# An eighth set of block products in a hybrid decoder layer: the first branch's other merge gates, and where the partner halves stand

## The chip, the core and the metric

The kernel runs on one core of one Trainium2 chip. The time is device microseconds (us) of one execution. A core has TensorE (PE, with its weight loads as PEld), VectorE (DVE), ScalarE (ACT), GpSimd (POOL) and SyncE (SP), each with an instruction queue of its own that it works off in order, and 16 DMA engines that all queues share. DMAs are issued from the queues of SP and POOL here, a few from ACT.

## The reference

One decoder layer over 256 tokens of width 2048, all in float32:

```python
h = rmsnorm(x, pre_norm_g)
proj = h @ w_in                       # 2048 x 18448
(a_q, a_k, a_v, a_g, a_lr, b_q, b_k, b_v, b_g, m_a, m_b) = split(proj)
gk  = log_sigmoid(a_lr @ gla_gk_w2 + gla_gk_b) / 16
o_a = gla_chunked(a_q, a_k, a_v, gk)              # gated linear attention, 4 heads
y_a = (rmsnorm(o_a, gla_norm_g) * silu(a_g)) @ w_branch_a
o_b = diff_attention(b_q, b_k, b_v, lam)          # 16 heads, two softmaxes each
y_b = (rmsnorm(o_b, diff_norm_g) * 0.8 * silu(b_g)) @ w_branch_b
merged = sigmoid(m_a) * y_a + sigmoid(m_b) * y_b
x = x + rmsnorm(merged @ w_out, post_norm_g)
```

`m_a` and `m_b` are the merge gates of the first and the second branch, 2048 columns each.

## The kernel before

**Splitting.** Nearly all the work is weights streamed from HBM against resident activations. Every weight tile comes in halves of 128x1024. For each half ACT writes a rounded copy `hi` (line 261), DVE the remainder `lo` (line 262), and PE multiplies `hi` by both parts of the activations and `lo` by the first. `hi` and `lo` have three buffers each; `take` lets ACT and DVE run three halves ahead of PE (`AHEAD`), in the order of one list, `seq`.

**Three kinds of half.** A plain token-major half (`half_tile`, 512 columns) is 12 matmuls of 512 columns. A channel-major half (`half_channel`) is 8 matmuls of 512 and 8 of 256 columns. Half of a block product is 6 matmuls of 512 columns.

**Sets of block products.** Seven groups of 1024 columns (`set0` to `set6`) are multiplied as 2x2 blocks by seven products in place of eight (`block_products`): the tokens in two blocks of 128, the 2048 rows of the weights in two of 1024, the columns in two of 512. The products run in the order 1, 3, 5, 6, 2, 7, 4, each in two steps t = 0, 1 of two halves: 14 steps or 28 halves a set. Sums of activation blocks are made once. Sums of weight blocks are made per set, in the tiles `chain[s, "a", t]` and `chain[s, "b", t]` of 1 MiB each:

- `link` loads a and b. Four buffers serve them, so the next set's a0 waits until DVE has read b0 in step (7,0), its a1 for step (7,1), b0 for (4,0) and b1 for (4,1). All but the first set's are issued from POOL (line 175).
- After step (1,t) has been split, an accumulating DMA from POOL (line 198, 512 KB) adds another weight block to each half of a[t]. Steps (5,0) and (5,1) need that sum.
- In steps (5,1), (6,0), (2,1), (7,0) DVE adds b or a third block `c` to a (line 206), and after (5,1) and (6,0) a second accumulating DMA adds to b, for product 7.
- The `c` tiles, four of 512 KB a set, are loaded by SP (line 190) ahead of product 2.

Finished gates leave the core to DRAM (`spill`, tiles `gr` and `gl`, line 129).

**Partner halves.** Between the steps stand halves of other projections, `others()`: the last value columns `v4`, then q and k of the first branch, then q and k of the second one's head groups (`dq`, `dk`) for the groups in `EARLY`, at most one half after a step (two in four steps of set 0). `phase_steps` writes this list; it leaves 14 steps without a partner, product 2's and 4's first steps in sets 1 to 6 and product 6's in sets 1 and 2. Each partner tile (`raw`, 1 MiB, two halves) is loaded by SP into one of three buffers (line 224). The time of this phase of sets is 85 to 593 us of the profile.

**After the phase** come the gates of the first branch (`ag0` to `ag3`), the first branch's merge gates `m02` and `m03` as plain groups of 512 columns around head group 3's channel-major halves (`diff_heads(3)`), then the two branch matrices and the output matrix. The attention of both branches runs as generators (`tasks`) that `pump` advances between these halves.

**Order.** The instructions of the phase's matmuls are pinned (`keep_in_program_order`); elsewhere a scheduler may move an instruction within its engine's queue, the fetches from DRAM among them (`fetch` line 134, `place` line 951).

Of the kernel before, what the change touches and what calls it, by code (L numbers as in the profile page):

```python
# [10 lines left out]
AF = mybir.ActivationFunctionType  # L11
# [3 lines left out]
P = 128  # L15
# [9 lines left out]
LANES = 3  # L25
# [1 line left out]
ROWS = {"two": 2, "tok": 4, "chan": KT}  # L27
WARM = 8
PRODUCTS = (1, 3, 5, 6, 2, 7, 4)
SETS = 7  # L30
MERGE = (0, 1, 6)
LEAD = 6
EARLY = (0, 1, 2)
BIG = 18
MORE = 13
BRIDGE = 512
# [3 lines left out]
def chunk_plan():  # L40

    plan = [("v0", "two", "w_in", [(6144, RANK), (2048, 2 * VG[0] - RANK)])]
    at = 2 * VG[0] - RANK
    for g, n in enumerate(VG[2:]):
        plan.append((f"v{g + 2}", "tok", "w_in", [(2048 + at, n)]))
        at += n
    for hf in range(2):
        for name, base in (("k", 1024), ("q", 0)):
            for c in range(4):
                plan.append((f"{name}{hf}{c}", "chan", "w_in", [(base + 512 * hf + P * c, P)]))  # L50
    o = 6144 + RANK
    for s in range(2):
        plan.append((f"set{s}", "set", "w_in", [(o + 10240 + 1024 * s, 1024)]))
    for s in range(2, 6):
        plan.append((f"set{s}", "set", "w_in", [(o + base + 512 * (s - 2), 512) for base in (4096, 6144)]))
    plan.append(("set6", "set", "w_in", [(o + 8192, 1024)]))
    for g in range(4):
        plan.append((f"ag{g}", "tok", "w_in", [(4096 + 512 * g, 512)]))
        for c in range(4):
            for n, name in enumerate(("dq", "dk")):  # L60
                plan.append((f"{name}{g}{c}", "chan", "w_in", [(o + 2048 * n + 512 * g + P * c, P)]))
        if g > 1:
            plan.append((f"m0{g}", "tok", "w_in", [(o + 8192 + 512 * g, 512)]))
        for br in range(2):
            plan.append((f"y{br}{g}", "tok", ("w_branch_a", "w_branch_b")[br], [(512 * g, 512)]))
        plan.append((f"o{g}", "tok", "w_out", [(512 * g, 512)]))
    return plan
# [9 lines left out]
def phase_steps():  # L77

    keys = ["v4"] + [f"{name}{hf}{c}" for hf in range(2) for name in ("k", "q") for c in range(4)]
    keys += [f"{name}{g}{c}" for g in EARLY for pair in range(2) for name in ("dq", "dk") for c in (2 * pair, 2 * pair + 1)]  # L80
    other = [(key, r, h) for key in keys for r in range(4 if key == "v4" else 1) for h in range(2)]
    slots = [(s, prod, t) for s in range(SETS) for prod in PRODUCTS for t in range(2)]
    front = [(0, prod, t) for prod in PRODUCTS[:2] for t in range(2)]
    skip = [(s, prod, 0) for prod in (2, 4, 6) for s in range(1, SETS)]
    skip = skip[: len(slots) + len(front) - len(other)]
    mixed = []
    for slot in slots:
        mixed += [("set", *slot, h) for h in range(2)]
        for _ in range((slot not in skip) + (slot in front)):
            mixed.append(other.pop(0))  # L90
    return mixed + other
# [3 lines left out]
def hybrid_kernel(ctx: ExitStack, tc, xt, xn, preg, postg, w, w2, gkb, glag, lamv, diffg, ident_d, causal_d, lmask_d, out):  # L95
    nc = tc.nc
    pe, act, dve, pool, sp = nc.tensor, nc.scalar, nc.vector, nc.gpsimd, nc.sync
# [28 lines left out]
    def spill(t, name):  # L126
        count[0] += 1
        d = dram.tile(list(t.shape), t.dtype, name=f"{name}_{count[0]}")
        pool.dma_start(d, t)
        return d  # L130

    def fetch(d, name, make, queue=pool):
        t = make(list(d.shape), name, d.dtype)
        queue.dma_start(t, d)
        return t

    def ps(tag):
# [3 lines left out]
    def f32(ap):  # L141
        return ap.bitcast(F32)
# [10 lines left out]
    def halves_of(*keys):  # L153
        return [(key, r, h) for key in keys for r in range(len(at[key])) for h in range(2)]

    def heads_order(g):
        return halves_of(*(f"{name}{g}{c}" for pair in range(2) for name in ("dq", "dk") for c in (2 * pair, 2 * pair + 1)))

    seq = halves_of("v0", "v2", "v3") + phase_steps()
    seq += halves_of(*(f"ag{g}" for g in range(4)))  # L160
    seq += halves_of("m02") + heads_order(3) + halves_of("m03", *(f"y0{g}" for g in range(4)))
    seq += halves_of(*(f"{name}{g}" for name in ("y1", "o") for g in range(4)))
    ready = {}
    emitted = [0]
# [13 lines left out]
    def emit_set(s, prod, t, h):  # L178
        c = slice(1024 * h, 1024 * h + 1024)
        if h == 0 and s + 1 < SETS and (prod, t) in ((7, 1), (4, 0)):  # L180
            link(s + 1, "a", 1 - t)
        if h == 0 and s + 1 < SETS and (prod, t) == (4, 1):
            link(s + 1, "b", 0)
# [161 lines left out]
    half_rstd = const.tile([P, 2], F32, name="half_rstd")  # L345
# [53 lines left out]
    ts, heads, m0 = {}, {}, []  # L399
# [63 lines left out]
    def token_major(key, n, ops, step=1, settle=None):  # L463
        banks = [ps("mm"), ps("mm")]
        for q in range(KT // 2):
            if settle:
                settle(q)
            half_tile(banks, n, q, ops, *take(key))
            if q % 2 or not ts:
                pump(step)  # L470
            else:
                pump_eager()
        return banks
# [179 lines left out]

    gspill = [None] * (2 * SETS)

    def merge_gate(banks):
        t = u2([P, 2, 512], "mgate")
        for b in range(2):
            act.activation(t[:, b, :], banks[b], AF.Tanh, scale=half_rstd[:, b : b + 1])
        m0.append(spill(t, "mgate"))  # L660

    def head_part(t, o, o2, scaled):
        act.activation(t, o2, AF.Copy)
        dve.tensor_tensor(out=t, in0=o, in1=t, op=ALU.add)
# [115 lines left out]

    sets = (step for s in range(SETS) for step in block_products(s))
    rest = others()
# [165 lines left out]
    obh, obl, values = [], [], {}  # L948

    def place(t, d, m, h):  # L950
        sp.dma_start(f32(t[64 * h : 64 * h + 64, m]), d[64 * m : 64 * m + 64])

    waiting = [(g, pair) for g in range(4) for pair in range(2)]

# [139 lines left out]
    for g in range(4):  # L1094
        banks = token_major(f"ag{g}", 512, x_ops, LANES)
        t = u2([P, 2, 512], "ua")
# [4 lines left out]
    def diff_heads(g):  # L1101
        for pair in range(2):
            for name in ("dq", "dk"):
                t = t2([P, 2, S], name)
                for c in range(2):
                    head_part(t[:, c, :], *channel_major(f"{name}{g}{2 * pair + c}"), name == "dk")
                    pump(LANES)
                heads[g, pair, name] = split_spill(t)
# [7 lines left out]
    def b_ops(kt):  # L1116
        return obh[kt // 4][:, kt % 4, :], obl[kt // 4][:, kt % 4, :]

    m0.extend(gspill[12:14])
    merge_gate(token_major("m02", 512, x_ops, LANES))  # L1120
    diff_heads(3)
    merge_gate(token_major("m03", 512, x_ops, LANES))

    while "out" not in done:
        pump(LANES)
# [1 line left out]
    for g in range(4):  # L1127
        part = fetch(m0[g], "part", u)
        banks = token_major(f"y0{g}", 512, a_ops, LANES)
# [29 lines left out]
    for g in range(4):  # L1159
        banks = token_major(f"y1{g}", 512, b_ops, 1 if g else LANES, None if g else settle)  # L1160
        for b in range(2):
            t = gb[g][:, b, :]
# [51 lines left out]
    for g in range(3):  # L1214
        banks = token_major(f"o{g}", 512, m_ops)
# [88 lines left out]
```

## Time and profile before

| | us |
|---|---|
| median of 3 runs (lowest, highest) | 1107.81 (1106.69, 1108.84) |
| the profiled execution, and its span | 1113.69, 1111.9 |
| PE busy | 1095.0 of the span (98%) |
| DVE, ACT, POOL busy | 863.4, 680.5, 132.3 |
| DMA: bytes moved, mean rate | 274.57 MB, 247 GB/s |

The profiled execution took 5.9 us more than the median run. Shares of busy time are means over the whole span; the rows for single stretches are shown with the prediction. A row of a group reads: line, engine, operation, written tile, read tiles, shapes, count, then busy us, mean ns of one, then the idle time before and what ended it.

### The profile page before, as it was taken

Reading aid. Unit: us, or ns where it says so; the run is one execution under the profiler, and the core shown is the slowest. Engines: PE = TensorE matmul, PEld = TensorE weight load, DVE = VectorE, ACT = ScalarE, POOL = GpSimd, SP = SyncE. Lnnn points to the kernel's source line nnn. Section 1 sums busy time; section 2 is a strip of 40 time slices with the busy share of each in tenths; the row PEclk is TensorE's granted clock in tenths of the full one; section 3 lists DMA queues with packets and bytes.
Section 4 is the critical chain, followed back from the end, with each engine's and each line's share of the span. In section 5 each row is a group of like instructions: output and inputs, shape, how many; then the busy total and the mean of one; then the engine's idle time right before and its main releaser. Section 6 shows DMA issues by size and latency. Waiting matters only on the chain.

```text
span 1111.9 us, 15248 instructions
## 1 busy us (share of the span) xinstructions
PE 1095.0 (98%) x5522; PEld 939.9 (85%) x5522; DVE 863.4 (78%) x1200; ACT 680.5 (61%) x989; POOL 132.3 (12%) x201
## 2 busy tenths in 40 slices
PE   8999999999999999999999999999999999999997
PEld 7999888888888888888887788888888888888886
DVE  6787987979979899798895998668877765656463
ACT  7895766666666666676664655557776653444460
POOL 0101112121121211213111000110110010000000
PEclk9999999999999999999999899999999999999999
DMA  8869969798897997988977445886888675556752
GB/s 329 296 225 325 297 241 319 204 309 222 285 298 204 340 252 264 314 211 317 269 244 249 146 160 187 271 277 228 273 288 243 206 260 189 190 189 212 272 197 76
DMA packets 58268, 274.57 MB, mean 247 GB/s; under 512 B 7824, under 2 KB 9360, under 8 KB 39248
## 3 DMA queue, kind: packets, MB, share of 16 engines
q1 hardware_dynamic: 36192, 184.18, 47.0%
q0 software_dynamic: 20992, 88.09, 28.6%
q10 hardware_dynamic: 1008, 1.32, 0.4%
q8 instruction: 43, 0.70, 0.2%
q14 instruction: 33, 0.27, 0.1%
HBM read 248.40 MB, written 25.17 MB: 246 GB/s over the span
## 4 chain that ended last, share of the span: by engine, by line
PE 94%; DMA 1%; issue 1%; ACT 1%; DVE 1%; POOL 0%; DVEq 0%; SPq 0%; POOLq 0%; ACTq 0%
PE mm L449 62%; PE bg L449 21%; PE bg L437 2%; PE mm L422 2%; PE mm L437 2%; PE bg L862 1%; DMA dl<-dk 1%; PE bg L422 1%; PE bg L996 1%; PE bg L997 1%; DMA raw<-in_w_dram 0%; PE bg L1021 0%; DVE lo L262 0%; PE bg L1034 0%; PE bg L1033 0%
## 5 line engine op out<-in xcount | busy, mean ns | idle before, releaser
L261 ACT ACTIVATE hi<-raw 128x1024 fp32r<-128x1024 f32 (+3 forms) x275 | 282.7, 1030 | 271.0 <-PE mm L449 168.3
L262 DVE TENSOR_TENSOR lo<-raw,hi 128x1024 fp32r<-128x1024 f32 (+3 forms) x275 | 325.9, 1188 | 145.1 <-ACT hi L261 142.0
L449 PE MATMUL mm<-hi,xs 128*128 128x512 f32 (+1 forms) x848 | 216.4, 389 | 4.2 <-ACT hi L261 4.2
L449 PEld LDWEIGHTS mm<-hi,xs 128*128 128x128 f32 x848 | 158.1, 190 | 31.3 <-ACT hi L261 5.0
L449 PE MATMUL bg<-xs,hi 128*128 128x512 f32 x640 | 164.9, 389 | 0.0
L262 DVE TENSOR_TENSOR lo<-a,hi 128x1024 fp32r<-128x1024 f32 x112 | 135.1, 1220 | 10.8 <-ACT hi L261 9.4
L449 PEld LDWEIGHTS bg<-xs,hi 128*128 128x128 f32 x640 | 120.3, 188 | 23.4
L261 ACT ACTIVATE hi<-a 128x1024 fp32r<-128x1024 f32 x112 | 118.7, 1060 | 29.8 <-PE mm L449 24.7
L449 PE MATMUL mm<-lo,xs 128*128 128x512 f32 (+1 forms) x424 | 119.0, 386 | 0.1
L449 PEld LDWEIGHTS mm<-lo,xs 128*128 128x128 f32 x424 | 79.6, 189 | 15.6 <-DVE lo L262 1.0
L449 PEld LDWEIGHTS bg<-xs,lo 128*128 128x128 f32 x640 | 87.3, 190 | 6.2
L449 PE MATMUL bg<-xs,lo 128*128 128x256 f32 x640 | 89.2, 282 | 0.0
L262 DVE TENSOR_TENSOR lo<-b,hi 128x1024 fp32r<-128x1024 f32 x56 | 67.3, 1221 | 7.0 <-ACT hi L261 6.2
L261 ACT ACTIVATE hi<-b 128x1024 fp32r<-128x1024 f32 x56 | 59.2, 1060 | 18.1 <-PE mm L449 15.8
L449 PE MATMUL mm<-hi,oah 128*128 128x512 f32 x128 | 50.9, 397 | 0.0
L449 PE MATMUL mm<-hi,obh 128*128 128x512 f32 x128 | 50.4, 394 | 0.0
L449 PE MATMUL mm<-hi,oal 128*128 128x512 f32 x128 | 50.0, 391 | 0.0
L449 PE MATMUL mm<-hi,obl 128*128 128x512 f32 x128 | 49.9, 390 | 0.0
L1007 ACT ACTIVATE prob<-prob,mx,score_scale 128x128 f32<-128x128 f32 x64 | 34.2, 536 | 13.2 <-DVE mx L1002 13.0
L198 POOL DMA_DIRECT2D b<-in_w_dram x28 | 24.4, 870 | 140.7 <-DVE a L206 127.7
L261 ACT ACTIVATE hi<-c 128x1024 fp32r<-128x1024 f32 x28 | 29.6, 1060 | 13.4 <-PE mm L449 6.8
L449 PE MATMUL mm<-hi,mh 128*128 128x512 f32 x96 | 37.5, 390 | 0.0
(288 smaller groups left out, 1882.3 us busy)
## 6 DMA issues: line engine op xcount, KB each, us to landing
raw<-in_w_dram SPq DMA_DIRECT2D x120, 1024.0 KB, 5.4
a<-in_w_dram POOLq DMA_DIRECT2D x28, 512.0 KB, 14.1
c<-in_w_dram SPq DMA_DIRECT2D x28, 512.0 KB, 8.9
b<-in_w_dram POOLq DMA_DIRECT2D x28, 512.0 KB, 7.7
a<-in_w_dram POOLq DMA_DIRECT2D x12, 1024.0 KB, 5.8
b<-in_w_dram POOLq DMA_DIRECT2D x12, 1024.0 KB, 8.9
raw<-in_w_dram SPq DMA_DIRECT2D x14, 832.0 KB, 6.9
dh<-dh POOLq DMA_DIRECT2D x16, 256.0 KB, 4.1
```

Source lines behind the costliest of these rows:

```text
L198: pool.dma_start(chain[s, name, i][:, c], weights(f"set{s}", 2 + i)[0][:, c], accum_op=ALU.add)
L261: act.activation(hi_t[:, a:b], r[:, a:b], AF.Copy)
L262: dve.tensor_tensor(out=lo_t[:, a:b], in0=r[:, a:b], in1=f32(hi_t[:, a:b]), op=ALU.subtract)
L422: i = pe.matmul(out, lhs, rhs, start=first and n == 0, stop=last and n == len(pairs) - 1)
L437: i = pe.matmul(banks[g][b][:, :n], a[part][:, P * b : P * b + P], w[:, n * g : n * g + n], start=first, stop=last)
L449: i = pe.matmul(*args, **kw)
L862: pe.matmul(o, xk[:, P * c : P * c + P], xq.rearrange("p (b c t) -> p b c t", b=2, c=4)[:, :, c, :], start=i == 0, stop=i == 1)
L996: pe.matmul(banks[m][:, lo:up], q2[:, m, i2, t], kh[:, m, i2, :n], start=True, stop=False)
L997: pe.matmul(banks[m][:, lo:up], q2[:, m, i2, t], kl[:, m, i2, :n], start=False, stop=True)
L1007: act.activation(prob[m][:, lo:up], prob[m][:, lo:up], AF.Exp, scale=score_scale[:, b : b + 1], bias=mx[:, i : i + 1], accum_out=z[:, i : ...
```

## The change

An eighth set takes the columns of `m02` and `m03`, 1024 columns, and these leave the tail as plain groups. Head group 2 leaves `EARLY`: its 16 channel-major halves move from the phase, where they were partners, to the tail, as `diff_heads(2)` behind `ag3`. The list of steps without a partner is rewritten: 44 of 112 steps, in sets 1 to 7 (1,0), (1,1), (3,0), (3,1), (5,0) and (4,0), and in set 7 also (7,1) and (4,1). Fetches and `place` are pinned to program order.

```diff
-SETS = 7
-MERGE = (0, 1, 6)
+SETS = 8
+MERGE = (0, 1, 6, 7)
-EARLY = (0, 1, 2)
+EARLY = (0, 1)
...
-    plan.append(("set6", "set", "w_in", [(o + 8192, 1024)]))
+    for s in range(6, SETS):
+        plan.append((f"set{s}", "set", "w_in", [(o + 8192 + 1024 * (s - 6), 1024)]))
...
-    skip = [(s, prod, 0) for prod in (2, 4, 6) for s in range(1, SETS)]
+    skip = [(SETS - 1, prod, t) for prod, t in ((7, 1), (4, 0), (4, 1))]
+    skip += [(s, prod, t) for prod, t in ((4, 0), (1, 0), (3, 0), (3, 1), (1, 1), (5, 0)) for s in range(SETS - 1 - (prod == 4), 0, -1)]
     skip = skip[: len(slots) + len(front) - len(other)]
...
     def fetch(d, name, make, queue=pool):
-        queue.dma_start(t, d)
+        tc.keep_in_program_order(queue.dma_start(t, d))
...
-    seq += halves_of("m02") + heads_order(3) + halves_of("m03", *(f"y0{g}" for g in range(4)))
+    seq += heads_order(2) + heads_order(3) + halves_of(*(f"y0{g}" for g in range(4)))
...
     def place(t, d, m, h):
-        sp.dma_start(f32(t[64 * h : 64 * h + 64, m]), d[64 * m : 64 * m + 64])
+        tc.keep_in_program_order(sp.dma_start(f32(t[64 * h : 64 * h + 64, m]), d[64 * m : 64 * m + 64]))
...
-    m0.extend(gspill[12:14])
-    merge_gate(token_major("m02", 512, x_ops, LANES))
+    m0.extend(gspill[12:16])
+    diff_heads(2)
     diff_heads(3)
-    merge_gate(token_major("m03", 512, x_ops, LANES))
```

What this does to the queues is shown at three places. The first is DVE from step (1,1) of the last set but one of the changed kernel, set 6, which is the last set before. `lo` rows that read `a` or `b` are block products, those that read `raw` are partners, rows on `dq` and `dk` are partners' results, a row L206 adds two blocks. Before:

```order
L262 TENSOR_TENSOR lo_4769<-a_4638,hi_4768 128x1024
L262 TENSOR_TENSOR lo_4780<-a_4638,hi_4779 128x1024
L671 TENSOR_TENSOR dq_4570<-dq_4570,dh_4760 128x512
L262 TENSOR_TENSOR lo_4793<-raw_4722,hi_4792 128x1024
L262 TENSOR_TENSOR lo_4813<-b_4667,hi_4812 128x1024
L262 TENSOR_TENSOR lo_4825<-b_4667,hi_4824 128x1024
L262 TENSOR_TENSOR lo_4837<-raw_4822,hi_4836 128x1024
L664 TENSOR_TENSOR dk_4790<-bg_4791,dk_4790 128x256
L262 TENSOR_TENSOR lo_4861<-b_4709,hi_4860 128x1024
L666 TENSOR_TENSOR dk_4790<-dk_4790,rstd_bc 128x256
L262 TENSOR_TENSOR lo_4871<-b_4709,hi_4870 128x1024
L262 TENSOR_TENSOR lo_4882<-raw_4822,hi_4881 128x1024
```

The same engine from the same step, now:

```order
L262 TENSOR_TENSOR lo_4296<-a_4196,hi_4295 128x1024
L658 TENSOR_TENSOR dq_4224<-bg_4225,dq_4224 128x256
L262 TENSOR_TENSOR lo_4320<-a_4196,hi_4319 128x1024
L262 TENSOR_TENSOR lo_4331<-b_4226,hi_4330 128x1024
L262 TENSOR_TENSOR lo_4341<-b_4226,hi_4340 128x1024
L262 TENSOR_TENSOR lo_4351<-b_4268,hi_4350 128x1024
L262 TENSOR_TENSOR lo_4364<-b_4268,hi_4363 128x1024
L262 TENSOR_TENSOR lo_4374<-a_4142,hi_4373 128x1024
L206 TENSOR_TENSOR a_4142<-a_4142,b_4226 128x1024
L262 TENSOR_TENSOR lo_4384<-a_4142,hi_4383 128x1024
L262 TENSOR_TENSOR lo_4396<-a_4196,hi_4395 128x1024
L262 TENSOR_TENSOR lo_4413<-a_4196,hi_4412 128x1024
```

Twelve rows ran from (1,1) to the partner of (3,1); they now reach the end of (5,1)'s block halves, with no partner among them.

The second place is SP's queue around the third blocks of set 2. Before:

```order
L190 DMA c_2447<-in_w_dram 128x1024
L190 DMA c_2463<-in_w_dram 128x1024
L224 DMA raw_2367<-in_w_dram 128x2048
L224 DMA raw_2461<-in_w_dram 128x2048
L224 DMA raw_2621<-in_w_dram 128x2048
L224 DMA raw_2702<-in_w_dram 128x2048
L190 DMA c_2499<-in_w_dram 128x1024
L190 DMA c_2513<-in_w_dram 128x1024
```

Now:

```order
L224 DMA raw_2287<-in_w_dram 128x2048
L224 DMA raw_2376<-in_w_dram 128x2048
L224 DMA raw_2469<-in_w_dram 128x2048
L190 DMA c_2272<-in_w_dram 128x1024
L190 DMA c_2289<-in_w_dram 128x1024
L190 DMA c_2313<-in_w_dram 128x1024
L190 DMA c_2327<-in_w_dram 128x1024
L224 DMA raw_2563<-in_w_dram 128x2048
```

The four `c` tiles of a set, which stood in two pairs with partner loads between, stand together behind one set's third partner load, which waits for the buffer of the partner of step (4,1) one set earlier; in sets 1 and 3 it is the same, and from set 4 on they stand behind the set's first partner load.

The third place is POOL at the end of the phase: the q and k of the first branch are fetched back, `vback` is its values, `gr` and `gl` are the last set's gates, `dh` and `dl` head parts. Before:

```order
L134 DMA vback_6296<-vh_538 128x1024
L134 DMA vback_6298<-vl_540 128x1024
L129 DMA gr_5292<-gr_5121 128x1024
L134 DMA vback_6300<-vh_775 128x1024
L129 DMA gl_5368<-gl_5200 128x1024
L824 MEMSET suf_5444 128x1024
L134 DMA vback_6302<-vl_777 128x1024
L129 DMA dh_5396<-dh_5393 128x512
L129 DMA dl_5398<-dk_5203 128x512
```

Now:

```order
L129 DMA gr_5282<-gr_5091 128x1024
L129 DMA dh_5256<-dh_5253 128x512
L129 DMA dl_5258<-dk_5094 128x512
L134 DMA q_5284<-q_2074 128x1024
L134 DMA k_5286<-k_1582 128x1024
L134 DMA q_5288<-q_3120 128x1024
L134 DMA k_5290<-k_2598 128x1024
L129 DMA gl_5337<-gl_5186 128x1024
L818 MEMSET suf_5383 128x1024
```

The last head parts stood behind four fetches of `vback` and the last gate's spill; they now stand ahead of the fetches of q and k, and `vback` is fetched later.

More of the change, by code (lines that the diff above doesn't have):

```diff
@@ L61, in chunk_plan @@
                 plan.append((f"{name}{g}{c}", "chan", "w_in", [(o + 2048 * n + 512 * g + P * c, P)]))
-        if g > 1:
-            plan.append((f"m0{g}", "tok", "w_in", [(o + 8192 + 512 * g, 512)]))
         for br in range(2):
@@ L654, in hybrid_kernel @@
     gspill = [None] * (2 * SETS)
[L656 to L660, printed above, removed]
     def head_part(t, o, o2, scaled):
```

## The prediction, made before the changed kernel ran

> **What bounds the kernel now.** I read the page's head, its chain, the chain in order of time, then busy time by stretches and the DMAs of one stretch.
>
> ```profile
> span 1111.9 us, 15248 instructions
> PE 1095.0 (98%) x5522; PEld 939.9 (85%) x5522; DVE 863.4 (78%) x1200; ACT 680.5 (61%) x989; POOL 132.3 (12%) x201
> ...
> PE 94%; DMA 1%; issue 1%; ACT 1%; DVE 1%; POOL 0%; DVEq 0%; SPq 0%; POOLq 0%; ACTq 0%
> ```
>
> PE is the pace: 98% busy and 94% of the chain. So removed matmuls count in full wherever nothing else takes over. In the chain in order of time, pieces without idle time give the prices of PE's work:
>
> ```profile
> 116.47 2.77 PE bg L449 x16
> 119.23 2.75 PE mm L449 x12
> ...
> 628.69 5.47 PE mm L449 x24
> ...
> 735.59 5.60 PE mm L449 x32
> ```
>
> A partner half costs 2.77 us, a step of a set 2.75, two plain halves in the tail 5.47, two channel-major ones there 5.60.
>
> The mean hides what stands beside PE in the phase. From the moment when b0 is free (`lo` of step (7,0) ended, the next set's first load is issued) to the landing of the last block that is added into a1, and from there to the next such moment, the six sets after the first give these rows (PE, PEld, DVE, ACT, POOL busy, clock, DMA share, GB/s), the first kind above the dots, the second below:
>
> ```profile
> core 0: us, PE busy (x) PEld busy (x) DVE busy (x) ACT busy (x) POOL busy (x), PEclk, DMA share, GB/s
> 146.10:191.70 45.60, 45.60 (x234) 38.96 (x234) 33.61 (x34) 29.10 (x33) 8.14 (x12) 1.00 0.92 306
> 218.20:257.20 39.00, 39.00 (x195) 33.15 (x195) 29.83 (x33) 26.89 (x31) 6.73 (x10) 1.00 0.93 304
> 288.30:329.60 41.30, 41.30 (x209) 35.22 (x208) 33.21 (x32) 27.04 (x30) 8.24 (x12) 1.00 0.96 315
> 359.80:400.70 40.90, 40.90 (x208) 34.90 (x207) 33.53 (x34) 27.00 (x31) 8.79 (x13) 1.00 0.99 326
> 431.00:474.00 43.00, 43.00 (x217) 36.63 (x216) 35.43 (x37) 28.66 (x33) 8.94 (x14) 1.00 0.97 307
> 503.10:544.70 41.60, 41.60 (x211) 35.47 (x210) 34.26 (x34) 27.69 (x32) 8.86 (x13) 1.00 0.98 321
> ...
> 191.70:218.20 26.50, 26.50 (x133) 22.57 (x132) 26.41 (x27) 17.65 (x20) 3.14 (x4) 1.00 0.75 188
> 257.20:288.30 31.10, 31.10 (x157) 26.27 (x157) 31.07 (x32) 19.98 (x23) 4.01 (x5) 1.00 0.76 220
> 329.60:359.80 30.20, 30.20 (x153) 25.57 (x152) 30.20 (x34) 20.85 (x25) 4.92 (x7) 1.00 0.77 205
> 400.70:431.00 30.30, 30.30 (x154) 25.73 (x153) 30.30 (x33) 21.33 (x25) 4.97 (x8) 1.00 0.81 211
> 474.00:503.10 29.10, 29.10 (x149) 24.65 (x148) 29.10 (x33) 19.77 (x23) 4.80 (x7) 1.00 0.77 207
> 544.70:573.70 29.00, 29.00 (x148) 24.74 (x147) 29.00 (x32) 20.26 (x25) 7.40 (x12) 1.00 0.75 189
> ```
>
> Each set has a DMA leg of 39 to 46 us in which the DMA engines are 92 to 99% busy, and a DVE leg of 26 to 31 us in which DVE is 100% busy. They follow each other by data: the loads wait for `lo` of (7,0), DVE's rest waits for the landing. PE never waits in either. How narrowly, set 6 shows; the rows are POOL's issues, ACT's instructions and an issue's time to landing:
>
> ```profile
> 503.38 0.55 POOL L175 DMA_DIRECT2D a<-in_w_dram  x1 [0.57 <-DVE lo L262]
> ...
> 527.95 0.92 POOL L198 DMA_DIRECT2D a<-in_w_dram  x1
> ...
> a<-in_w_dram POOLq DMA_DIRECT2D x1, 512.0 KB, 16.7
> ...
> 544.87 2.12 ACT L261 ACTIVATE hi<-a 128x1024 fp32r<-128x1024 f32 x2
> ```
>
> The last added block lands at 527.95 + 16.7 = 544.7. The two `hi` are those of step (5,1); the second, which needs this block, begins at 545.9. The margin is 1.2 us after a leg of 41.6.
>
> **The matmuls.** The set is 14 steps, 14 x 2.75 = 38.5 us. `m02` and `m03` are 16 plain halves, 8 x 5.47 = 43.8. Head group 2's 16 halves leave the phase (16 x 2.77 = 44.3) and cost 8 x 5.60 = 44.8 in the tail. Together 38.5 - 43.8 - 44.3 + 44.8 = -4.8 us. The attention's generators get as many calls of `pump` beside the tail's halves (the plain groups gave 8, `diff_heads(2)` gives 8). What covers the rest, by stage:
>
> ```profile
> 116.50:589.00 472.50, 472.50 (x2375) 402.15 (x2374) 418.50 (x426) 316.07 (x356) 83.44 (x122) 1.00 0.87 267
> ...
> 613.00:725.00 112.00, 111.66 (x538) 94.25 (x539) 96.18 (x130) 62.13 (x83) 6.97 (x12) 0.97 0.59 193
> ...
> 790.00:914.00 124.00, 122.93 (x659) 105.22 (x658) 91.89 (x275) 82.42 (x210) 15.62 (x25) 1.00 0.78 258
> ```
>
> The set's 28 `hi` cost ACT 30 us, where it idles 156 in the phase. Head group 2's eight spills and its matmuls move to the tail, where DMA, ACT and POOL have room; the attention's second half gets these heads later, but before it asks for them (group 0 and 1 come first), so 0. Without that cover it would be a wait on POOL as at the phase's end, some 7 us.
>
> **The phase's end.** Here PE waits now:
>
> ```profile
> 601.54 9.44 DMA dl<-dk
> ...
> 613.34 8.50 PE mm L449 x24
> ...
> ACT xq L835 <- DMA dl<-dk: 9.5, 1, 9.5
> ...
> 609.40:613.30 3.90, 0.09 (x1) 0.00 (x0) 1.48 (x3) 2.17 (x4) 0.00 (x0) 0.88 0.03 12
> 613.30:621.90 8.60, 8.56 (x25) 6.80 (x26) 8.57 (x12) 3.92 (x5) 0.97 (x2) 0.66 0.35 121
> ```
>
> ACT stands 9.5 us before `xq`, whose memory a head part still leaves; the spill of that part had queued on POOL behind `vback`. PE loses 3.9 us, and then 24 matmuls take 8.50 us in place of 5.47, at a granted clock of 0.66. Now the last head part is made three steps earlier and its spill stands ahead of the fetches: I take both losses away, -6.9 us. Late next are q and k, fetched behind it, but three plain halves (8.2 us) are then converted. If a like wait comes back, this term is 0. The other pinned fetches can no longer run ahead; bounded by that wait, between 0 and +6.9, I take 0, since in the stretch with most idle time behind it (790 to 914 us, above) PE loses 1.1 us in all.
>
> **The legs.** From the same moment to the `hi` of (5,1)'s second half took 545.9 - 503.1 = 42.8 us of PE's pace. Five partner halves now leave that stretch, after (1,0), (1,1), (3,0), (3,1), (5,0): 5 x 2.77 = 13.9, so PE comes for the block after 28.9 us. Does the DMA leg shrink as much? What it moved in set 6, with each queue's share of the 16 engines in 41.6 us:
>
> ```profile
> q0 software_dynamic: 1681, 8.13, 65.7%
> q1 hardware_dynamic: 854, 5.18, 31.6%
> ...
> raw<-in_w_dram SPq DMA_DIRECT2D x4, 1024.0 KB, 8.2
> ...
> b<-in_w_dram POOLq DMA_DIRECT2D x2, 1024.0 KB, 10.8
> a<-in_w_dram POOLq DMA_DIRECT2D x4, 512.0 KB, 14.4
> c<-in_w_dram SPq DMA_DIRECT2D x2, 512.0 KB, 7.9
> ```
>
> POOL's queue took 27.3 us (four links, four added blocks, two gates, a pair of head parts), and all of it stays. SP's took 13.1 us for 5.18 MB, 2.66 us per MiB. A partner load is issued when a partner tile is done with, so of four two remain, those behind (7,0) and (4,1). In sets 4 to 7 `c` stands behind a load that waits for (2,0)'s partner, ahead of the leg: 27.3 + 2 x 2.66 + 0.8 (the 2% idle) = 33.4 us (38.7 if it slips in). In sets 2 and 3 all four `c`, 2 MiB, fall into it: 38.7. In set 1 one of its partner loads goes, 45.6 - 2.7 = 42.9.
>
> The DVE leg keeps what it has and gets one partner more (two in sets 1 and 2), while the margin at its start falls away. At 1.22 us a `lo` (row below) against a margin of 1.2 that is 29.7 us, the mean of the last four rows; in sets 1 to 3 I take 28.8, that of the first two.
>
> Legs in series against PE's own pace for a set, 14 x 2.75 + 8 x 2.77 = 60.7 (63.5 to set 1, with one partner more): set 1, 71.7 - 63.5 = 8.2; sets 2 and 3, 67.5 - 60.7 = 6.8 each; sets 4 to 7, 63.1 - 60.7 = 2.4 each. Sum 31.4 us. The waits at the blocks are longer (33.4 - 28.9 = 4.5 in sets 4 to 7), but PE gets part back in the DVE leg, which is shorter than its own 31.8. Bounds: at 326 GB/s, the best row, and with a DVE leg of 29.0, sets 4 to 7 move 8.13 + 2.10 = 10.2 MB in 31.4 us and lose nothing, the others some 16 in all; if the DMA leg shrinks in no set, 7 x (41.6 + 29.7 - 60.7) = 74. I take 31.4, near the low end, because the queue's shares are counted and the loads that go are known.
>
> **Sum:** -4.8 - 6.9 + 31.4 = +19.7: the profiled execution's 1113.7 (span 1111.9 and 1.8 around it) would be 1133.4. The median of the runs shown lies 5.9 under it, so 1107.8 + 19.7 = 1127.5 us.
>
> **Rivals.**
> *The blocks arrive in time.* A share near 1 may be a queue that is kept full rather than a limit. Then PE's pace holds: 1107.8 - 11.7 = 1096.1 us, faster. It decides at a DMA leg of 60.7 - 29.7 = 31.0 us. For it: PE has not waited once, and sets 4 to 7 miss it by 2.4. Against: six legs in a row at 92 to 99%.
> *DVE is the pace, and the blocks arrive.* To 418.5 us of DVE in 472.5 come 28 + 8 - 16 operations of 1.22, less some 8 for heads: 435 of 467, 93%. A loss of 1 us a set gives 1103.
>
> ```profile
> L262 DVE TENSOR_TENSOR lo<-a,hi 128x1024 fp32r<-128x1024 f32 x112 | 135.1, 1220 | 10.8 <-ACT hi L261 9.4
> ```
>
> *Each wait lowers the clock.* The wait of 3.9 us above cost 3.0 more. Seven such, one a set, add 21: 1148 us. Against: the blocks land one by one, a half of matmuls between. The Trainium skill (TensorE: Matmul & The Clock Gate, "HAM oscillation") says that DMA waits of more than about 3.4 us between bursts leave the next burst at half the clock each time. By that rule this rival is the likelier the longer a single wait is; the 0.66 after 3.9 us agrees with it.
> *The legs shrink further than I count,* and it comes out even: 1108.
>
> **How the numbers follow.** Waits as counted 0.61 (own range 1112 to 1143), blocks in time 0.13, DVE 0.06, lowered clock 0.14, even 0.06. The likeliest gives 1127. The range 1102 to 1149 leaves out most of the blocks in time and the top of the lowered clock, under 0.2. Faster by over 0.2%, about what a measurement can tell: 0.20; within: 0.04; slower: 0.76.
>
> **What would show it.** ACT's `hi` waiting for DMA `a` and `b` in the list of waits, some 4 us a set and 10 in sets 1 to 3; PE idle in the phase, nowhere at its end; DMA legs of 33 to 43 us at shares above 0.9, with PE's share below 1; a set's period of 63 to 71 us in place of 71.6; no `xq` behind `dl`. PE busy 1.00 through the phase would prove me wrong, a clock below 1 in sets 1 to 3 would make it worse.

## The result, and the profile after

The changed kernel takes 1154.8 us (median of 4 runs, 1152.5 to 1156.1), the kernel before beside it 1107.9; the ratio is 1.040, 95% interval 1.038 to 1.043. That is slower, as forecast, but by 47 us where 20 were forecast, and 6 us above the range. The profiled execution took 1152.5, span 1150.8. Its page and its chain:

```profile
span 1150.8 us, 15255 instructions
PE 1107.7 (96%) x5498; PEld 935.4 (81%) x5498; DVE 887.5 (77%) x1224; ACT 691.8 (60%) x1003; POOL 140.6 (12%) x213
...
PE 80%; DMA 12%; DVE 4%; issue 2%; ACT 1%; POOL 0%; DVEq 0%; SPq 0%; POOLq 0%; ACTq 0%
```

PE carried 94% of the chain before; DMA has now 12 in place of 1, and DVE 4 in place of 1. In the list of waits ACT stands where the prediction put it, before the `hi` of blocks:

```profile
ACT hi L261 <- DMA a<-in_w_dram: 50.7, 25, 5.3
...
ACT hi L261 <- DMA b<-in_w_dram: 8.1, 4, 3.2
```

Busy time by stretches, cut at the same moments as before: from the issue of the next set's a0 to the landing of the last block added into a1 (the rows above the dots, sets 1 to 7), and from there to the next a0 (below, six times). The last row adds all of them up, and the 38.7 us behind the last landing.

```profile
core 0: us, PE busy (x) PEld busy (x) DVE busy (x) ACT busy (x) POOL busy (x), PEclk, DMA share, GB/s
144.70:187.40 42.70, 38.01 (x178) 31.15 (x177) 28.91 (x29) 24.89 (x28) 8.14 (x12) 0.96 0.92 293
216.10:258.20 42.10, 35.92 (x162) 28.45 (x161) 28.18 (x27) 22.98 (x26) 8.15 (x12) 0.93 0.94 297
287.90:327.90 40.00, 34.31 (x158) 27.85 (x157) 28.57 (x28) 22.66 (x25) 8.13 (x12) 0.95 0.95 307
356.90:392.60 35.70, 34.12 (x161) 28.01 (x160) 28.32 (x27) 22.69 (x26) 8.16 (x12) 1.00 0.97 304
423.70:460.20 36.50, 33.30 (x152) 25.87 (x150) 27.95 (x28) 22.00 (x25) 8.66 (x13) 1.00 0.96 286
490.40:526.90 36.50, 34.15 (x156) 26.68 (x155) 28.94 (x29) 22.85 (x26) 8.69 (x13) 1.00 0.94 287
556.20:593.30 37.10, 34.65 (x160) 27.40 (x158) 28.51 (x28) 22.96 (x26) 8.69 (x13) 1.00 0.95 289
...
187.40:216.10 28.70, 28.62 (x137) 23.73 (x136) 27.33 (x27) 18.91 (x21) 2.55 (x3) 0.94 0.57 139
258.20:287.90 29.70, 29.70 (x142) 24.85 (x141) 28.49 (x30) 19.36 (x21) 2.56 (x3) 0.93 0.53 127
327.90:356.90 29.00, 28.63 (x139) 23.76 (x138) 27.82 (x28) 19.21 (x21) 2.56 (x3) 0.95 0.72 193
392.60:423.70 31.10, 30.03 (x147) 24.45 (x147) 29.77 (x31) 20.72 (x23) 3.75 (x6) 1.00 0.75 210
460.20:490.40 30.20, 29.99 (x142) 24.66 (x143) 28.81 (x30) 19.97 (x23) 3.72 (x5) 0.94 0.73 204
526.90:556.20 29.30, 28.20 (x139) 22.91 (x140) 28.13 (x29) 19.65 (x22) 3.72 (x5) 1.00 0.76 210
...
sum 487.30, PE 456.76 PEld 370.16 DVE 405.75 ACT 304.55 POOL 81.19; mean PE 32.63 PEld 26.44 DVE 28.98 ACT 21.75 POOL 5.80
```

PE stood still for 1.6 to 6.2 us in every DMA leg, and for 30.5 in all these stretches, where it had not stood once before. The second stretches are at most 1.4 us longer than forecast. The first ones, but for set 1's, miss it by more:

| set | 1 | 2 | 3 | 4 | 5 | 6 | 7 |
|---|---|---|---|---|---|---|---|
| DMA leg, forecast | 42.9 | 38.7 | 38.7 | 33.4 | 33.4 | 33.4 | 33.4 |
| DMA leg, measured | 42.7 | 42.1 | 40.0 | 35.7 | 36.6 | 36.4 | 37.1 |
| second stretch, forecast | 28.8 | 28.8 | 28.8 | 29.7 | 29.7 | 29.7 | |
| second stretch, measured | 28.8 | 29.7 | 29.0 | 31.1 | 30.2 | 29.4 | |

DMA legs here and below run from a0's issue to the landing. What moved in the leg of set 5, by queue, with the rate in 40 slices:

```profile
GB/s 5 153 242 431 395 278 404 395 269 368 368 180 72 359 359 224 350 427 391 418 413 404 364 395 346 251 202 184 198 211 283 373 256 224 216 215 215 180 211 215
...
q0 software_dynamic: 1712, 8.32, 81.2%
q1 hardware_dynamic: 292, 2.10, 15.0%
...
a<-in_w_dram POOLq DMA_DIRECT2D x4, 512.0 KB, 14.0
```

POOL's queue (`q0`) took 0.812 x 36.5 = 29.6 us here, where 27.3 were counted; SP's (`q1`) took 5.5, where 5.3 were, and for 1.4 us the engines served neither, where 0.8 was counted. In the leg's last third, where adds run almost alone, the rate is mostly 180 to 224 GB/s, though the DMA engines count as busy for 0.96 of the leg. Where loads run it is mostly 350 to 430.

### The profile page after: what moved, and what is told of

It reads as the page before. It is cut to its first block, busy times and chain, and to the rows that moved or that the text cites. A ratio compares the mean times of both kernels' runs of the same rounds, so it can differ in the third digit from the quotient of the medians.

```text
span 1150.8 us, 15255 instructions
## 1 busy us (share of the span) xinstructions
PE 1107.7 (96%) x5498; PEld 935.4 (81%) x5498; DVE 887.5 (77%) x1224; ACT 691.8 (60%) x1003; POOL 140.6 (12%) x213
## 3 DMA queue, kind: packets, MB, share of 16 engines
q0 software_dynamic: 22720, 96.48, 31.1%
## 4 chain that ended last, share of the span: by engine, by line
PE 80%; DMA 12%; DVE 4%; issue 2%; ACT 1%; POOL 0%; DVEq 0%; SPq 0%; POOLq 0%; ACTq 0%
PE mm L449 55%; PE bg L449 14%; DMA a<-in_w_dram 11%; DVE lo L262 2%; PE bg L437 2%; PE mm L422 2%; PE mm L437 2%; ACT hi L261 1%; PE bg L856 1%; DVE a L206 1%; PE bg L422 1%; PE bg L990 1%; PE bg L991 1%; DMA raw<-in_w_dram 0%; PE bg L1015 0%
## 5 line engine op out<-in xcount | busy, mean ns | idle before, releaser
L262 DVE TENSOR_TENSOR lo<-raw,hi 128x1024 fp32r<-128x1024 f32 (+3 forms) x259 | 306.0, 1184 | 114.8 <-ACT hi L261 111.6
L262 DVE TENSOR_TENSOR lo<-a,hi 128x1024 fp32r<-128x1024 f32 x128 | 155.3, 1222 | 62.1 <-ACT hi L261 60.3
L449 PE MATMUL mm<-hi,xs 128*128 128x512 f32 (+1 forms) x768 | 195.0, 386 | 2.2 <-DVE gr L767 1.8
L261 ACT ACTIVATE hi<-a 128x1024 fp32r<-128x1024 f32 x128 | 135.4, 1059 | 98.0 <-DMA a<-in_w_dram 50.7
L449 PE MATMUL bg<-xs,hi 128*128 128x512 f32 x512 | 132.2, 390 | 0.0
L449 PEld LDWEIGHTS bg<-xs,hi 128*128 128x128 f32 x512 | 96.5, 189 | 19.1
L449 PEld LDWEIGHTS bg<-xs,lo 128*128 128x128 f32 x512 | 69.3, 190 | 8.7 <-DVE lo L262 4.0
L449 PE MATMUL bg<-xs,lo 128*128 128x256 f32 x512 | 72.0, 284 | 1.5 <-DVE lo L262 1.4
L449 PE MATMUL mm<-xs,hi 128*128 128x512 f32 x256 | 67.5, 396 | 0.0
L449 PE MATMUL mm<-hi,r1h 128*128 128x512 f32 x64 | 31.3, 489 | 25.9 <-ACT hi L261 25.7
L449 PEld LDWEIGHTS mm<-xs,hi 128*128 128x128 f32 x256 | 46.2, 189 | 7.7
```

Source lines behind the costliest of these rows:

```text
L261: act.activation(hi_t[:, a:b], r[:, a:b], AF.Copy)
L262: dve.tensor_tensor(out=lo_t[:, a:b], in0=r[:, a:b], in1=f32(hi_t[:, a:b]), op=ALU.subtract)
L449: i = pe.matmul(*args, **kw)
```

## Experiments

Times are medians; "before" is the kernel before, run beside them (1107.9 to 1110.9). Each edit is to the changed kernel unless the kernel before is named.

**The phase's end, the pins.** First, the kernel before once more, with no edit.

> The kernel before once more, nothing changed. Its shown profile took 1113.7, 5.9 over the median of its other runs, and lost 3.9 us idle and 3.0 of clock at the phase's end. Theory A (that stall is in every execution, the 5.9 are elsewhere): this profile shows ACT xq behind dl and a PE gap of 3 to 5 us near 609 again, the time is 1107 to 1109. Theory B (the stall was the chance of that one execution, and the sum took away a loss that the median never had): no gap over 1 us at the phase's end, span near 1106, and xq not behind dl.

Measured: 1109.7, ratio 0.9995 (0.998 to 1.001), span 1106.8. Its list of waits has

```profile
ACT xq L835 <- DMA dl<-dk: 7.7, 1, 7.7
```

and PE stands 2.0 us at 607 us, not 3.9. The stall is in this execution too, at half the size; its first leg also began 2.1 us earlier than in the profile shown (144.3 against 146.4). Neither theory holds whole: the place was right, the size differs between executions (2.0 and 3.9 us).

The kernel before with the pins:

```diff
-        queue.dma_start(t, d)
+        tc.keep_in_program_order(queue.dma_start(t, d))
```

and the same in `place`.

> The kernel before with the pins alone (fetch and place in program order): vback no longer stands ahead of the last head part on POOL, everything else is as before, the phase's sets too. If the stall at the phase's end is in every execution and the pins take it away: 1101 (1107.8 - 6.9), no xq behind dl. If it was a chance of one execution: 1107 to 1109. If the pins cost something in the attention: up to 1112, with PE gaps after 780 us.

Measured: 1106.6, ratio 0.998 (0.996 to 0.9997). PE has no gap at the phase's end, and what is left of that wait in the list of waits

```profile
ACT xq L835 <- DMA dl<-dk: 3.7, 1, 3.7
```

is covered by other work. The pins are worth about 2 us here, not 6.9. It is the one version whose interval lies under 1, and only just.

The changed kernel without the pins (the edit above, undone):

> The changed kernel without the pins: eight sets and the same steps without a partner, vback again ahead of gr, dh and dl on POOL. Waits in the phase as in the changed kernel (29 us of PE gaps). If the pins are worth what the stall showed: 1154.8 + 4 to 7 = 1159 to 1162 with xq behind dl. If the last head part, made earlier, is what matters: 1154 to 1156.

Measured: 1154.5, ratio 1.042 (1.038 to 1.046), no `xq` behind `dl`. There the pins do nothing: the last head part is made earlier, and that is enough. The two parts of the change are thus apart, and the loss lies in the phase of sets.

**The clock.** Around the wait of 3.9 us in set 1, PE's granted clock is half for 6.8 us, seen in stretches of 2 us with the same columns:

```profile
182.00:184.00 2.00, 0.12 (x1) 0.00 (x0) 0.00 (x0) 0.00 (x0) 0.00 (x0) 0.96 1.10 264
184.00:186.00 2.00, 0.00 (x0) 0.00 (x0) 0.00 (x0) 1.06 (x1) 0.00 (x0) 0.50 1.03 211
186.00:188.00 2.00, 1.96 (x5) 1.57 (x6) 1.23 (x1) 0.52 (x1) 0.00 (x0) 0.50 1.09 215
188.00:190.00 2.00, 2.00 (x6) 1.41 (x5) 1.43 (x2) 2.00 (x3) 0.00 (x0) 0.50 0.38 74
```

So the rival of the lowered clock is real as a mechanism. Whether it costs time:

```diff
+                    if s in (1, 2, 3) and (prod, t, h) == (5, 1, 0):
+                        spare = ps("bg")
+                        for _ in range(12):
+                            mm(spare, x_ops(0)[0][:, :P], x_pair(0), start=True, stop=True)
                     hi, lo = take(("set", s, prod, t, h))
```

> The changed kernel with 12 matmuls more in sets 1 to 3, ahead of step (5,1), into a bank that nobody reads: they run in the wait of some 4 us in which PE now stands, 12 x 0.23 = 2.7 us. Clock theory (each of those waits costs the clock 0.50 for 6 to 8 us, and this is part of the loss): the clock stays at 1.00 there and the kernel gains 3 to 4 us a set, 1144 to 1146. Leg theory (the set is paced by the DMA leg and then by DVE's leg, and PE's slow matmuls lie beside DVE's): 1153 to 1156, though the clock stays up and PE's idle time moves to waits for lo after (5,1).

Measured: 1159.0, ratio 1.045 (1.041 to 1.050). In set 1:

```profile
186.00:188.00 2.00, 1.90 (x6) 0.97 (x6) 1.23 (x1) 0.53 (x1) 0.00 (x0) 1.00 1.09 217
...
187.40:217.40 30.00, 27.92 (x136) 22.28 (x137) 28.45 (x28) 18.62 (x21) 2.56 (x4) 1.00 0.53 132
```

The clock stays at 1.00, and the second stretch is not shorter but 30.0 us (28.7 in the changed kernel): PE now stands 2.1 us there, 1.2 of them in one wait for `lo`. One thing is mixed in: the scheduler put two of DVE's additions (line 206) ahead of the `lo` of (6,0), whose first half comes 2.3 us later by it. So the run does not show what a full clock alone would give. The rows above bound it: DVE works 27.3 of 28.7, 28.5 of 29.7 and 27.8 of 29.0 us in these stretches of sets 1 to 3, so as long as it has the same to do there, a faster PE can shorten each by 1.2 to 1.4 us at most.

**Where the free steps stand.**

```diff
-    ... ((7, 1), (4, 0), (4, 1))]   ... ((4, 0), (1, 0), (3, 0), (3, 1), (1, 1), (5, 0)) ...
+    ... ((7, 1), (4, 0), (4, 1))]   ... ((7, 0), (2, 0), (2, 1), (6, 0), (6, 1), (5, 1)) ...
```

> The changed kernel with the same number of partners a set, but the six free steps behind the block: (5,1), (6,0), (6,1), (2,0), (2,1), (7,0). Leg theory (a set lasts DMA leg + DVE leg): in the DMA leg PE has its partners again, about 41 us of matmuls against a leg of 38 to 42, so no gap at the blocks; DVE's leg loses five partners' lo, 29.7 - 5 x 1.22 = 23.6, and PE now waits there for lo. A set lasts 63 to 66 in place of 71.4, 71.8, 69.0, 66.8, 66.8, 65.8: some 20 us less in all, 1135 (1125 to 1142). Rival (a set with 8 partners loses the same wherever they stand): 1150 to 1157.

Measured: 1134.4, ratio 1.022 (1.020 to 1.025). No `hi` waits for a DMA `a`. Set 5, the two stretches:

```profile
411.10:446.30 35.20, 34.51 (x173) 28.77 (x173) 27.44 (x27) 22.45 (x26) 7.87 (x12) 1.00 0.92 285
446.30:477.40 31.10, 28.42 (x126) 21.64 (x125) 30.29 (x32) 20.74 (x24) 4.65 (x6) 1.00 0.78 218
```

The block lands after 35.2 us, before PE comes for it, and now DVE is busy for 30.3 of 31.1 us while PE waits for `lo`. Twenty us came back, as worked out from the leg theory, and a second limit took the place of the first. In sets 1 to 3 the split is near the theory's too (legs of 42 to 45 us, second stretches of 22 to 25). In sets 4 to 6 it is not: legs of 35.2 to 35.8 and second stretches of 29.9 to 31.1 stand where 38 to 42 and 23.6 were expected, so that part of the agreement is luck.

**What fills the DMA leg.** The third blocks on another queue:

```diff
-            sp.dma_start(raws[s, i, j], ...)
+            tc.keep_in_program_order((act if s else sp).dma_start(raws[s, i, j], ...))
```

> The changed kernel with the third blocks c issued from ACT's queue at their place in the program, from step (5,0) on, in place of SP's: they leave the DMA legs of sets 1 to 3 (2 MiB each) and what slips into those of sets 4 to 7. If bytes of SP count in the leg as the prediction priced them (2.66 us a MiB): legs of sets 1 to 3 fall to about 37, 4 to 5 us each, 1 us in the others, 1137 to 1143. If SP's bytes pass beside POOL's queue, which is the limit: legs as before, 1151 to 1156.

Measured: 1148.5, ratio 1.034 (1.031 to 1.037). The legs of sets 1 to 3 fall from 42.7, 42.1, 40.0 to 39.3, 37.4, 36.3; those of 4 to 7 become 36.9 to 38.0 (35.7 to 37.1), since part of `c` now comes at the leg's end. It lies between the two expectations, but the legs of sets 1 to 3 speak for the first. ACT's queue still moved half a MiB of `c` within each leg, in set 2

```profile
q10 hardware_dynamic: 140, 0.52, 3.6%
```

so some 1.5 of the 2 MiB left it, for 3.4 to 4.6 us: 2.3 to 3.1 us a MiB, about the 2.66 that the prediction counted. What the kernel gained less than expected is the half MiB that now stands in the legs of sets 4 to 7.

The spill of `gl` behind the adds:

```diff
-                            gspill[2 * s] = spill(halves["l"], "gl")
+                            held.append((s, halves["l"]))
+                    if held and (prod, t, h) == (3, 0, 1):
+                        flush()          # gspill[2 * s] = spill(tile, "gl"), of the set before
```

> The changed kernel with each set's spill of gl (512 KB, in POOL's queue between the adds of a0 and a1) issued after the next set's step (3,0), behind all four adds; the last set's as before. If what stands in POOL's queue ahead of the last add sets the leg's end: 1.3 us a set, seven sets 9 us, 1144 to 1148. If the leg is set by when the last add is issued or by single transfers: 1153 to 1156.

Measured: 1145.9, ratio 1.033 (1.031 to 1.035). What stands in POOL's queue ahead of the last add sets the leg's end: 512 KB there cost 8 to 9 us in seven sets.

The adds as copies:

```diff
-            pool.dma_start(chain[s, name, i][:, c], ..., accum_op=ALU.add)
+            pool.dma_start(chain[s, name, i][:, c], ..., **({} if name == "a" else dict(accum_op=ALU.add)))
```

> The changed kernel with the two blocks that are added into a (line 198) written as plain copies of the same bytes, on the same queue and in the same order, so that products 5 and 6 use the block alone and not the sum: only the kind of transfer differs. In the legs' last part, where adds run almost alone, the trace shows 207 to 216 GB/s at a DMA share above 0.99, against 390 to 440 where loads run. If adding is what makes them slow: four of 512 KB a set at about 2.5 us fall to 1.3, legs 4 to 5 us shorter, seven sets 25 to 30 us, 1125 to 1130. If the rate there is that of POOL's queue or of few bytes in flight: 1151 to 1156.

Measured: 1121.7, ratio 1.010 (1.007 to 1.013), 33 us less than the changed kernel. Legs 37.5, 37.0, 35.2, 31.1, 32.3, 31.6, 32.5, that is 4.2 to 5.2 us shorter; set 4:

```profile
342.40:373.50 31.10, 31.10 (x150) 26.17 (x149) 26.35 (x26) 22.75 (x26) 5.95 (x11) 1.00 0.88 339
373.50:404.30 30.80, 30.80 (x156) 25.98 (x155) 30.62 (x32) 20.28 (x23) 4.63 (x7) 1.00 0.80 213
```

The records of single packets say why: a packet of 4 KB takes 327 ns when it adds and 160 ns when it copies.

The same edit in the kernel before:

> The kernel before with the same edit as the changed kernel had in the run with copies: the two blocks that are added into a are written as copies, products 5 and 6 use the block alone. There the edit gave 33 us. If the kernel before is paced by PE and its legs have room: legs 4 to 5 us shorter, the sets' periods as before (70 to 72 us), 1106 to 1111, no change. If its legs were the limit too: 1080 to 1090.

Measured: 1109.2, ratio 0.999 (0.997 to 1.001). Its legs fall to 33 to 40 us, and the sets' periods stay at 72.1, 70.1, 71.5, 71.3, 72.0, to 0.1 us those of the other profiles of before. What is worth 33 us with eight partners a set is worth nothing with twelve.

**The second stretch.** DVE's additions left out:

```diff
-        i = {(5, 1): 0, (6, 0): 1, (2, 1): 0, (7, 0): 1}.get((prod, t))
+        i = {(5, 1): 0, (6, 0): 1}.get((prod, t))
```

> The changed kernel without DVE's additions of the third blocks c to a (four a set, line 206 after steps (2,1) and (7,0)), so that product 4 uses a without them; the transfers stay. Two of the four stand in DVE's leg ahead of lo of (7,0), at 1.2 us each. Leg theory (the two legs stand in series and DVE's counts in full though PE works all through it): 2.4 us a set and some more behind it, six or seven sets, 1135 to 1141. Rival (only the DMA leg costs, DVE's leg lies beside PE's own work): 1151 to 1156.

Measured: 1156.6, ratio 1.042 (1.038 to 1.047). The expectation failed: the second stretches are 28.7 to 30.0 us, at most 1.1 us shorter, and some DMA legs are longer (46.0 us in set 1; why, no run shows). This edit and the 12 matmuls together:

> The changed kernel with both the 12 matmuls in the waits of sets 1 to 3, which kept the clock up, and without DVE's additions of c to a (product 4 uses a without them). Each alone gained nothing. If the stretch after the landing has two limits side by side, DVE's queue and a PE at half clock without its lead, only both together shorten it: 2 to 3 us in each of sets 1 to 3, 1147 to 1151. If a third thing sets it (single hi and lo of halves after a lost lead): 1155 to 1160.

Measured: 1157.7, ratio 1.043 (1.041 to 1.045); second stretches 29.3, 29.7, 29.3 in sets 1 to 3. Two parts of the stretch of set 1:

```profile
192.40:197.40 5.00, 3.80 (x21) 2.98 (x20) 5.00 (x6) 2.39 (x4) 1.71 (x2) 1.00 0.93 154
...
207.40:212.40 5.00, 5.00 (x27) 4.28 (x26) 2.83 (x3) 2.58 (x3) 0.00 (x0) 1.00 0.64 211
```

Five us behind the landing DVE is busy without a pause and PE waits 1.2 us for a `lo`, before which the scheduler again put two additions; 15 us later PE is busy without a pause, and DVE idles for 2.2 of 5 us. So in these runs the stretch has two limits one behind the other: without the additions of `c`, PE works 27.1 of its 29.3 us and DVE 24.3, and what either could still give is 2.2 us. My "DVE leg" is right as a length and wrong as a name.

**Together.** Free steps (3,1), (5,0), (5,1), (6,0), (2,0), (2,1), with `c` on ACT's queue and the later `gl`:

> Eight sets with what the runs so far point to: per set six partners in the DMA leg and two behind it, free steps (3,1), (5,0), (5,1), (6,0), (2,0), (2,1); c from ACT's queue; gl spilled behind the adds. Leg theory: DMA leg 34 to 36 beside 37 us of PE's work, DVE's leg 23.6 + 2 x 1.22 = 26, so 63 to 64 us a set against PE's own 60.7: 1134.4 of the run with all partners in the leg less 6 for set 1 and 2 to 3 for each other, 1118 (1112 to 1125), still slower than before. If c on ACT's queue or the later gl costs as much as it gives: 1130.

Measured: 1133.0, ratio 1.022 (1.018 to 1.026), 15 us more than expected. And with the copies too:

> The same, and the two blocks added into a written as copies as in the other run with copies, so that products 5 and 6 use the block alone: the eight sets with as few waits as these means reach. It measures what the matmuls' term was worth. Waits of 0 to 2 us a set: 1099 to 1112. If the change loses elsewhere than in the legs (the tail, the attention): 1115 or more.

Measured: 1133.0, ratio 1.021 (1.018 to 1.025): no difference, though the DMA legs are 3 to 7 us shorter. In set 5 of the first of the two:

```profile
411.00:446.00 35.00, 35.00 (x179) 29.83 (x178) 28.21 (x30) 23.92 (x28) 8.45 (x13) 1.00 0.99 307
446.00:477.00 31.00, 28.02 (x124) 21.38 (x123) 30.70 (x31) 20.20 (x22) 4.08 (x5) 1.00 0.76 211
```

PE waits only where DVE is busy for 30.7 of 31 us. In four of the six steps from (5,1) to (7,0) each half brings DVE a `lo` and an addition, 2.4 us against 1.4 of PE's matmuls; a partner there gives PE 2.77 us for one `lo` more, and I had taken four of them away. With the changed kernel's own free steps, the copies, `c` on ACT's queue and the later `gl`:

> The changed kernel, its free steps where they are, with the three things that each shortened the DMA leg taken together: the blocks added into a written as copies (products 5 and 6 use the block alone), gl spilled behind them, c issued from ACT's queue. If the waits at the blocks are the whole loss: legs of 29 to 32, PE's own pace of 60.7 to 62 us a set, 1107 to 1113, about the time before. If something else of the change loses: 1118 or more.

Measured: 1122.6, ratio 1.012 (1.010 to 1.014). No leg is over 34.0 us (29.2 to 31.8 from set 2 on), and from set 2 on a set still lasts 61.9 to 65.1 against PE's own 60.7. The stretch after the landing in set 4, in its first and its last part:

```profile
365.20:373.00 7.80, 6.65 (x28) 4.86 (x27) 7.73 (x8) 5.17 (x6) 2.62 (x3) 1.00 0.92 221
...
389.00:398.40 9.40, 9.40 (x51) 8.07 (x50) 9.40 (x11) 5.44 (x6) 0.00 (x0) 1.00 0.33 115
```

DVE is busy nearly without a pause, and of PE's gaps in the phase, some 13 us in all, 10.4 are waits for `lo`. So the waits at the blocks are some 32 us of the loss; with them nearly gone, DVE holds the sets back.

**The eighth set, or the partners?** The kernel before with the pins, seven sets, and head group 2 moved to the tail:

```diff
-EARLY = (0, 1, 2)
+EARLY = (0, 1)
-    skip = [(s, prod, 0) for prod in (2, 4, 6) for s in range(1, SETS)]
+    skip = [(s, prod, t) for prod, t in ((4, 0), (1, 0), (3, 0), (3, 1), (5, 0)) for s in range(1, SETS)]
...
+    diff_heads(2)
     diff_heads(3)
```

> Seven sets as before, with m02 and m03 as plain groups and the pins; only head group 2 goes to the tail, and five steps a set are left without a partner, (4,0), (1,0), (3,0), (3,1), (5,0), nine partners a set. PE's work is that of before and 0.5 us. Theory that the poor sets are the cause: PE's own pace is 14 x 2.75 + 9 x 2.77 = 63.4 us a set, the stretches one after the other 71 in sets 1 to 3 and 67 in sets 4 to 6: 7.5 x 3 + 4 x 3 = 34 more than before with the pins, 1141 (1128 to 1146). If the eighth set itself is what costs: 1106 to 1112.

Measured: 1132.2, ratio 1.020 (1.018 to 1.023); DMA legs 43.3, 40.6, 37.1, 38.0, 36.2, 36.9. Set 4:

```profile
352.00:390.00 38.00, 36.59 (x175) 30.21 (x173) 29.43 (x31) 25.16 (x29) 7.84 (x12) 1.00 0.97 321
390.00:420.00 30.00, 28.89 (x141) 23.50 (x142) 29.88 (x31) 19.63 (x23) 4.57 (x7) 1.00 0.78 209
```

Against the pins alone (1106.6) it loses 25.6 us without an eighth set. The sets that lost partners are the cause.

## Why the prediction was right and wrong

*Direction and place were right:* waits of ACT's `hi` for `a` and `b` between (5,0) and (5,1), PE idle in the phase, shares above 0.9 in the legs. *The matmuls' term* holds as far as the tail shows it. From the last `lo` of a set's `a` (588.3 before, 636.0 after) to the first matmul of `y0` (816.0 and 855.1 in these rows, before and then after)

```profile
L449 PE MATMUL mm<-hi,oah x128: 387/389/481, 816.0 to 923.4; 128*128 128x512 f32 x128
```

```profile
L449 PE MATMUL mm<-hi,oah x128: 387/390/482, 855.1 to 962.5; 128*128 128x512 f32 x128
```

it took 227.7 us and takes 219.1, that is some 8.7 less; the terms give -43.8 + 44.8 - 2.8 (the last partner, which stood behind that `lo`) - 6.9 = -8.7. From there to the end they take 295.9 and 295.7. The phase's own part of the term, 38.5 - 44.3, no run shows without waits.

*The phase's end* was right for the execution shown and too large for the kernel: 2 us by the pins in the kernel before. A small wait also came up, 1.8 us at 631 us, PE behind DVE's `gr` of product 7, where (7,1) of the last set has no partner now. I took the difference between the profiled execution and the median for a constant (5.9); part of what I credited stood in it. Profile against profile the change costs 38.9 us. The 46.9 of the medians are these, 5.8 by which the profile before lies over the median of the runs beside the changed kernel, and 2.3 by which the profile after lies under its own.

*The legs are the step that failed.* Up to the last `lo` of `a`, 47.7 us came on; the matmuls ahead of it are 38.5 - 44.3 + 2.8 = 3.0 fewer, so the waits are 50.7 us where the sum had 31.4. Of these 19.3, 16.7 are DMA legs, 2.7 second stretches (the table). These 19.3 and the 5.8 and 2.3 of the medians are the 27 us by which the forecast was short. The mis-sized term is the DMA leg, 27.3 (POOL's queue) + 2 x 2.66 (SP's two loads) + 0.8 (idle) in sets 4 to 7. There I struck 8.2 of 41.6 us, and 4.5 to 5.9 went. The legs by queue say which part is wrong. Set 2, where all of `c` runs beside the adds:

```profile
GB/s 0 140 335 420 436 397 374 319 428 362 276 101 389 86 342 381 420 272 335 335 358 300 276 288 269 288 261 269 288 389 401 378 265 276 284 276 237 234 206 195
...
q0 software_dynamic: 1693, 8.30, 67.7%
q1 hardware_dynamic: 864, 4.19, 25.9%
```

SP's 4.19 MB, 4.0 MiB, took 0.259 x 42.1 = 10.9 us, 2.7 us a MiB, and over the seven legs it is 2.5 to 2.7. So the price of 2.66 held, and SP's loads are not free beside the adds: where both run, the rate is 261 to 288 GB/s, between the 211 of adds alone and the 350 to 430 of loads. The Trainium skill (DMA: Bandwidth & Descriptors, "SWDGE vs HWDGE vs iDMA") says that transfers issued from GpSimd (POOL) and those issued from SP or ACT feed different queues inside each DMA engine, between which the engine takes turns; the rate between the two agrees with it.

Counted so in sets 2 to 7 together, POOL's queue took 170.5 us where the sum had 163.8, SP's 45.6 where it had 42.6 (2.1 to 2.7 MB in sets 4 to 7 and not 2.1), and for some 12 us the engines served neither, where it had 4.8. This idle time is 1.1 to 2.7 us a leg; the 0.8 was set 6's alone, though the prediction's own rows go down to a share of 0.92. And POOL's queue had more to move before the landing, the next add, into `b`, which set 5 issues 4.5 us ahead of it:

```profile
455.73 0.86 POOL L198 DMA_DIRECT2D b<-in_w_dram  x1 [9.93 <-DVE a L206]
```

What that leg's block needs (four links, four added blocks, two gates, a pair of head parts) is 7.86 MB, and the queue moved 8.32; the other 0.46 MB, an estimated 2.2 us at 211 GB/s, can only be that add's. So a leg lasts longer than its queues' work for the block, by time in which engines idle or already do what comes next. Why that time is longer now, no run takes apart. That an add takes twice a copy's time makes the legs as long as they are, as the run with copies shows, but it is not what the sum missed: set 6's 27.3 us held that time already.

*The row that was read too hopefully* is the 326 GB/s of the lower bound: with fewer of SP's loads, more of a leg's bytes are adds, and sets 4 to 7 moved 286 to 304 GB/s. The share does not show this: an engine counts as busy for the whole of an add's packet (0.97 at 304 GB/s in set 4, 0.88 at 339 with copies). *The rivals:* the clock fell as that rival said (0.61 stood against its 0.14), in five of the seven sets, yet the run with a full clock gained nothing, and the rows bound its worth at 1.2 to 1.4 us in each of sets 1 to 3. DVE as the pace was priced at 1 us a set from a mean of 93%; with the blocks in time it costs some 3, since from (5,1) to (7,0) DVE has hardly a pause. The range's top was the clock's price, and no bound of it came from legs that don't shrink, though 74 us stood in the text for that.

## What to carry to other kernels

A stretch in which PE never waits can be within a microsecond of two other limits; before taking its cover away, take the limits one at a time from the stretch itself, not from the mean. A queue's busy share held as a price of its bytes; what the sum lacked was room for time in which the engines idle or already work on the next transfer, so a stretch shortened by less than the bytes that left it. Such a term is better taken from the worst of the rows than from one good one. The cover that a partner gives counts by place, for the block's landing ahead of it and for DVE's additions behind it, and in none of the orders run here did eight partners a set do for both.

## What the runs showed of the hardware

An accumulating DMA from POOL takes 327 ns a packet of 4 KB and a copy on the same queue 160; alone the adds move about 211 GB/s at a DMA share of 1. Where adds and SP's loads run together in set 2, the rate is 261 to 288. PE's granted clock fell to 0.50 in set 1, 1.7 us into a wait of 3.9 us, and came back 4.6 us after it. It also fell, for 3.4 us, in sets 5 and 7, where no single wait is longer than 1.7 us; set 5:

```profile
457.00:459.00 2.00, 0.31 (x2) 0.12 (x2) 0.14 (x1) 1.06 (x1) 0.00 (x0) 1.00 1.12 203
459.00:461.00 2.00, 1.94 (x6) 0.93 (x6) 1.08 (x1) 0.67 (x1) 0.00 (x0) 0.83 0.79 154
461.00:463.00 2.00, 1.79 (x5) 1.27 (x5) 1.58 (x2) 2.00 (x3) 0.00 (x0) 0.50 0.05 10
```

In sets 4 and 6, with waits of 1.5 and 1.7 us, it stayed at 1.00. In set 2 it fell at 252.1, 1.6 us after a wait of 1.9 us and 0.7 us before one of 4.1 us began, so it is half while PE still works:

```profile
252.00:254.00 2.00, 0.79 (x2) 0.10 (x1) 0.00 (x0) 0.00 (x0) 0.00 (x0) 0.52 1.03 270
```

The rule that the prediction quotes from the Trainium skill (TensorE: Matmul & The Clock Gate, "HAM oscillation"), waits of more than about 3.4 us, fits sets 1 to 3 in so far as each has such a wait (3.9, 4.1 and 4.3 us) and lost the clock, though in sets 1 and 3 it fell 1.7 us into the wait. It covers neither set 2's early fall nor sets 5 and 7.
